# Delta rule: 32-row base inverse on GpSimd, one doubling level fewer on TensorE, and the second half's queries and keys projected earlier

## The chip, the cores and the metric

The kernel runs on one core of a Trainium2 chip. A core has TensorE (PE; its weight loads are listed as PEld), VectorE (DVE), ScalarE (ACT), GpSimd (POOL), a sync engine (SP) that issues most transfers, and 16 DMA engines. Each engine works through its own instructions in the order in which they stand and waits where a semaphore tells it to. The metric is the device time of one execution in microseconds; lower is better.

## The reference

Two transformer blocks in sequence over 256 tokens of width 2048, all in float32. The change lies in the second block's mixer, in its gated delta rule (8 heads of 128, token chunks of 64):

```python
A = jnp.where(tri_strict, jnp.einsum('bhnid,bhnjd->bhnij', kb, k) * decay, 0.0)
T = lax.linalg.triangular_solve(eye + A, jnp.broadcast_to(eye, A.shape),
                                left_side=True, lower=True)
u = jnp.einsum('bhnij,bhnjd->bhnid', T, v * beta[..., None])
w = jnp.einsum('bhnij,bhnjd->bhnid', T, kb * jnp.exp(G)[..., None])
...
v_new = u_i - jnp.einsum('bhck,bhkv->bhcv', w_i, state)
o_i = (jnp.einsum('bhck,bhkv->bhcv', q_i, state)
       + jnp.einsum('bhij,bhjv->bhiv', qk_i, v_new))
```

Here `q`, `k`, `v` come from one large projection `h @ w_in`, followed by a short causal convolution, silu and (for q and k) a norm; the delta rule's output is normed, gated, joined to the output of a block-sparse attention and multiplied by `w_out`.

## The kernel before

**Projections.** Every large matrix product goes through `linear` (L269). It splits each weight tile into a high and a low part (ACT L320, DVE L324) and adds three fp32r products of 128x512 (L295 to L297) for each of the two token halves. Weights stream from HBM through three buffers, issued by SP (L261, L265). The first token half is `LAG` units ahead of the second.

**Background work.** Everything small (convolutions, the delta rule, attention) is written as generators. `linear` advances them between its units: each `yield cost, wait` says how much of the budget a step takes and how long, on a planner's clock that counts projected columns, the lane must rest before its next step. `stat` of the last product `w_out` forces generators whose result it needs. The instructions then stand in a fixed order on each engine, so a background product on PE that is not ready holds back all projection products behind it.

**The delta rule.** Here the kernel treats 128 tokens as one chunk, and each half of the heads has four heads by two chunks, eight 128x128 lower triangular matrices to invert. `gdn(half)` makes convolutions of k and q, norms, then the masked products of k with k (`KE`, L1108 and L1109). `base_inverse` (L1017) inverts the diagonal blocks of 16 rows: POOL writes the blocks to a scratch in DRAM (eight transfers, L1025), reads them back with one block matrix per partition (`K`, 64 partitions of 16x16, L1034), scales them by `cb` (L1043), runs 15 elimination steps of two instructions (L1048, L1049) on `R`, writes `R` to DRAM (L1051) and reads it back into the diagonal of `T` (eight transfers, L1054). For each b in `LEVELS` = 16, 32, 64 a doubling level follows: POOL makes the mask `cm` (L1126), PE transposes `T` (8 matrices, L209 through `transpose8`), multiplies `KE` by `T` (L1131) and the transposed `T` by the masked result (L1137), and DVE subtracts (L1138). Then `finish(t)` gives the output of each token half: `head_norm` (ACT, DVE, ACT with a square root, DVE, POOL L1201 and L1203) and `tsplit` (four transposes on PE, L209).

**The order around it.** In `block2_mixer` (L1241) the projection calls, each 1024 columns wide, come as: q and k of half 0; v of half 0 and a gate; q and k of half 1; v of half 1 and attention queries; and so on to `w_out`. `gdn(0)` runs in lane 0 from the second of these on, `gdn_value(0)` (convolution and scaling of v) in lane 1 from the third on, and `gdn(1)` from the fourth on. `moba(half)` is the attention: its normed output goes through POOL L1201 as well. A row's line number shifts by one from L1048 on in the changed file.

Of the kernel before, what the change touches and what calls it, by code (L numbers as in the profile page):

```python
# [13 lines left out]
ALU = mybir.AluOpType  # L14
# [4 lines left out]
S, D, P = 256, 2048, 128  # L19
# [4 lines left out]
HP = 50  # L24
HPE = 30
HPL = 30
LEVELS = (16, 32, 64)
TWO_PI = 2.0 * math.pi


def constants():
# [8 lines left out]
    parts = [m > n, m <= n, m < n, np.ones((128, 128))]  # L40
    for b in LEVELS:
        c = np.arange(64)
# [100 lines left out]
class Net:  # L143
# [873 lines left out]
    def base_inverse(self, KE, cc):  # L1017

        nc = self.nc
        d1, d2 = self.scratch(64 * 256), self.scratch(64 * 256)  # L1020

        def view(d, b):
            return bass.AP(tensor=d.tensor, offset=d.offset + b * 256, ap=[[16, 16], [2048, 8], [1, 16]])
        for b in range(8):
            nc.gpsimd.dma_start(view(d1, b), KE[b * 16:b * 16 + 16, :, b * 16:b * 16 + 16])  # L1025
        tp = self.mis([P, P])
        nc.tensor.transpose(tp[:8, :], cc.rearrange("p t h -> p (t h)"), self.ident)
        cr = self.w2([8, P])
        nc.vector.tensor_scalar(cr, tp[:8, :], -1.0, None, op0=ALU.mult)
        yield 0.2, 4.0  # L1030
        cb = self.sm([64, 16], "cb", 1)
        nc.gpsimd.dma_start(cb, cr)
        K = self.w2([64, 16, 16])
        nc.gpsimd.dma_start(K.rearrange("p a b -> p (a b)"), bass.AP(tensor=d1.tensor, offset=d1.offset, ap=[[256, 64], [1, 256]]))  # L1034
        R = self.w2([64, 16, 16])
        Rf = R.rearrange("p a b -> p (a b)")
        e = nc.gpsimd
        e.memset(R, 0.0)
        e.memset(Rf[:, 0:256:17], 1.0)
        T = self.s4([P, 8, P])  # L1040
        e.memset(T, 0.0)
        yield 0.0, 4.0
        e.tensor_tensor(K, K, cb[:, None, :].to_broadcast([64, 16, 16]), op=ALU.mult)  # L1043
        yield 0.0, 1.0
        for m in range(15):
            sh = [64, 15 - m, m + 1]
            tmp = self.sm(sh, "btmp")
            e.tensor_tensor(tmp, K[:, m, m + 1:][:, :, None].to_broadcast(sh), R[:, m, :m + 1][:, None, :].to_broadcast(sh), op=ALU.mult)  # L1048
            e.tensor_tensor(R[:, m + 1:, :m + 1], R[:, m + 1:, :m + 1], tmp, op=ALU.add)  # L1049
        yield 0.0, 12.0  # L1050
        nc.gpsimd.dma_start(bass.AP(tensor=d2.tensor, offset=d2.offset, ap=[[256, 64], [1, 256]]), Rf)  # L1051
        yield 0.0, 3.5
        for b in range(8):
            nc.gpsimd.dma_start(T[b * 16:b * 16 + 16, :, b * 16:b * 16 + 16], view(d2, b))  # L1054
        yield 0.0, 4.5
        self.Tb = T

# [15 lines left out]
    def gdn(self, half, qraw, kraw, beta, decays, zs, at, box):  # L1073
# [48 lines left out]
        c8 = cc.rearrange("p t h -> p (t h)")[:, :, None].to_broadcast([P, 8, 64])  # L1122
        for li, b in enumerate(LEVELS):
            cm = self.w2([P, 8, 64])
# [115 lines left out]

    def block2_mixer(self):  # L1241
        nc, I = self.nc, self.I
        self.c2 = self.s4([P, 704])
        nc.sync.dma_start(self.c2, I["cst2"])
        parked = []
        stat = r = self.norm_split(self.piece, "mix", "rx", lambda x=self.x: parked.append(self.park(x)))
        self.piece = self.x = None
        w = I["w_in_2"][0]
        zs = [self.s4([P, 2, 512]) for _ in range(2)]
        ba = self.sm([P, 2, 16], "ba", 1)  # L1250

        def ev_z1(t, j, ps):
            if j == 0:
                nc.scalar.activation(zs[1][:, t, 0:264], ps, AF.Silu, scale=r[t])
                return
            nc.scalar.activation(zs[1][:, t, 264:512], ps[:, 0:248], AF.Silu, scale=r[t])
            nc.scalar.activation(ba[:, t], ps[:, 248:264], AF.Copy, scale=r[t])
        self.lpat = "v"
        self.linear(w, [(3584, 264), (3848, 264)], stat, ev_z1, carry=True)
        beta, g = self.gates(ba)  # L1260
        decays = {}
        bias = {}
        self.bg.add(self.moba_bias(bias), 1)
        self.bg.add(self.gdn_decay(0, g, decays), 0)
        oT = LazyAT(self)
        SC = 128.0 ** -0.5

        def to(*dst):
            def f(t, j, ps):
                d, kind = dst[j]  # L1270
                if kind == "t":
                    return self.channel_major(d, t, ps, r[t])
                elif kind == "q":
                    return self.channel_major(d, t, ps, r[t], SC)
                elif kind == "z":
                    nc.scalar.activation(d[:, t], ps, AF.Silu, scale=r[t])
                else:
                    nc.scalar.activation(d[:, t].rearrange("p h c -> p (h c)"), ps, AF.Copy, scale=r[t])
            return f

        def new():
            return self.s4([P, 4, S])
        q, k = new(), new()
        self.linear(w, [(0, 512), (1024, 512)], stat, to((q, "t"), (k, "t")), carry=True)
        box = {}
        self.bg.add(self.gdn(0, q, k, beta, decays, zs, oT, box), 0)
        v = new()
        self.linear(w, [(2048, 512), (3072, 512)], stat, to((v, "t"), (zs[0], "z")), budget=2.0, carry=True)
        self.bg.add(self.gdn_value(0, v, box), 1)
        q, k = new(), new()  # L1290
        self.linear(w, [(512, 512), (1536, 512)], stat, to((q, "t"), (k, "t")), budget=2.0, carry=True)
        box = {}
        self.bg.add(self.gdn_decay(1, g, decays), 0)
        self.bg.add(self.gdn(1, q, k, beta, decays, zs, oT, box), 0)
        v, mq = new(), new()
        self.linear(w, [(2560, 512), (4112, 512)], stat, to((v, "t"), (mq, "q")), budget=2.0, carry=True)
        self.bg.add(self.gdn_value(1, v, box), 1)
        mk, mv = new(), self.s4([P, 2, 4, P])
        self.linear(w, [(5136, 512), (6160, 512)], stat, to((mk, "t"), (mv, "v")), budget=2.0, carry=True)
# [287 lines left out]
```

## Time and profile before

| | us |
|---|---|
| median of 3 runs | 2434.64 |
| lowest and highest | 2433.32, 2436.43 |
| the profiled execution's own time | 2435.66 |
| its span | 2433.5 |
| PE busy | 2406.7 |
| DVE busy | 1553.0 |
| ACT busy | 1429.6 |
| POOL busy | 199.8 |

The profiled execution took 1.0 us more than the median, and 2.2 us lie outside its span. A busy time on PE is not the work itself: products are pipelined, and the distance from one start to the next is what a product costs. POOL is idle for most of the program, but the chain from `KE` to `T` runs through it.

### The profile page before, as it was taken

To read this page: it belongs to the slowest core of one execution; us is meant where nothing else is said; L and a number is where in the kernel's file an instruction comes from. 1 tells how busy PE (TensorE), PEld (TensorE's weight loads), DVE (VectorE), ACT (ScalarE), POOL (GpSimd) and SP (SyncE) were. 2 spreads that over 40 slices of the span, in tenths; PEclk is the share of its full clock that TensorE was granted. 3 is DMA by queue.
4 is the path that set the end of the run, shared out by engine and by line. 5 is a ranking of instruction groups with operands and counts; after the bars stand their busy time and mean duration, and the time that the engine had idled before them with its cause. 6 is when DMAs were issued, how large, how long until landed. Compare 5 with 4: busy or idle time off the path is not lost.

```text
span 2433.5 us, 32136 instructions
## 1 busy us (share of the span) xinstructions
PE 2406.7 (99%) x11363; PEld 1994.4 (82%) x11363; DVE 1553.0 (64%) x2842; ACT 1429.6 (59%) x2678; POOL 199.8 (8%) x217
## 2 busy tenths in 40 slices
PE   9999999999999999999999999999999999999998
PEld 7788878888888888888887888788888888888887
DVE  6998585555555666566758656576556556567754
ACT  7458675545545556466545555586565565566744
POOL 1740000000000000000301411000000000001000
PEclk9999999999999999999999999999999999999999
DMA  7546456555555666656444535645565555555553
GB/s 250 173 137 217 156 166 206 191 189 191 184 191 190 200 197 198 194 175 223 156 140 143 182 122 188 210 165 190 183 197 173 191 191 173 190 197 224 187 205 139
DMA packets 193569, 448.64 MB, mean 184 GB/s; under 512 B 12932, under 2 KB 17568, under 8 KB 193408
## 3 DMA queue, kind: packets, MB, share of 16 engines
q1 hardware_dynamic: 192192, 446.05, 55.1%
q8 instruction: 89, 1.46, 0.2%
q0 software_dynamic: 1216, 0.54, 0.1%
q14 instruction: 72, 0.59, 0.1%
HBM read 439.78 MB, written 6.75 MB: 183 GB/s over the span
## 4 chain that ended last, share of the span: by engine, by line
PE 90%; issue 3%; ACT 3%; DVE 2%; DMA 1%; POOL 0%; POOLq 0%; SPq 0%; ACTq 0%; DVEq 0%
PE acc L295 28%; PE acc L296 28%; PE acc L297 28%; PE mis L209 3%; ACT wh L320 1%; DVE wl L324 1%; DMA raw<-in_w_uq_dram 1%; PE mis L1108 0%; PE mis L1131 0%; PE mis L1137 0%; DVE s L984 0%; POOLq L1583 0%; ACT s L242 0%; ACT w L203 0%; DMA s<-in_mem_dram 0%
## 5 line engine op out<-in xcount | busy, mean ns | idle before, releaser
L324 DVE TENSOR_TENSOR wl<-raw,wh 128x512 fp32r<-128x512 f32 (+2 forms) x1574 | 1101.3, 708 | 763.3 <-ACT wh L320 759.1
L320 ACT ACTIVATE wh<-raw 128x512 fp32r<-128x512 f32 (+3 forms) x1640 | 1011.0, 625 | 859.4 <-DVE wl L324 480.1
L295 PE MATMUL acc<-wh,s 128*128 128x512 f32 (+3 forms) x3280 | 1284.1, 394 | 3.9 <-ACT w L555 2.0
L296 PE MATMUL acc<-wl,s 128*128 128x512 f32 (+3 forms) x3280 | 1269.9, 388 | 2.5 <-DVE wl L324 2.1
L297 PE MATMUL acc<-wh,s 128*128 128x512 f32 (+3 forms) x3280 | 1268.5, 388 | 0.2 <-DVE s L243 0.2
L295 PEld LDWEIGHTS acc<-wh,s 128*128 128x128 f32 x3280 | 617.5, 188 | 125.6 <-ACT s L242 5.6
L296 PEld LDWEIGHTS acc<-wl,s 128*128 128x128 f32 x3280 | 618.0, 188 | 123.1 <-DVE wl L324 6.8
L297 PEld LDWEIGHTS acc<-wh,s 128*128 128x128 f32 x3280 | 616.3, 188 | 125.1 <-DVE s L243 1.7
L515 DVE SCALAR_TENSOR_TENSOR s<-mis,cols,s 128x255 f32<-128x255 f32 (+29 forms) x240 | 93.1, 455 | 0.0
L324 POOL TENSOR_TENSOR wl<-raw,wh 128x512 fp32r<-128x512 f32 (+2 forms) x66 | 84.0, 1286 | 91.4 <-ACT wh L320 90.3
L1406 POOL TENSOR_TENSOR s<-s,s 128x1024 f32<-128x1024 f32 x11 | 32.7, 2975 | 663.2 <-ACT s L1405 663.2
L243 DVE SCALAR_TENSOR_TENSOR s<-mis,cols,s 128x128 fp32r<-128x128 f32 x212 | 66.4, 346 | 18.1 <-ACT s L242 16.2
L242 ACT ACTIVATE s<-mis,cols 128x128 fp32r<-128x128 f32 x212 | 69.6, 379 | 13.9 <-PE mis L209 7.9
L209 PE MATMUL mis<-c,w 128*128 128x128 f32 x456 | 71.9, 275 | 2.2 <-ACT w L1234 1.4
L209 PEld LDWEIGHTS mis<-c,w 128*128 128x128 f32 x456 | 56.4, 140 | 20.9 <-ACT w L1234 3.0
L209 PE MATMUL mis<-c,s 128*128 128x128 f32 x416 | 61.7, 277 | 4.3 <-DVE s L747 1.4
L209 PEld LDWEIGHTS mis<-c,s 128*128 128x128 f32 x416 | 50.2, 142 | 16.5 <-issue 2.6
L866 DVE TENSOR_TENSOR s<-s,s 128x512 fp32r<-128x512 f32 x88 | 58.9, 686 | 1.1 <-ACT s L865 1.1
L203 ACT ACTIVATE w<-s 128x512 f32<-128x512 f32 (+2 forms) x90 | 51.4, 573 | 8.5 <-DVE s L1436 6.2
L865 ACT ACTIVATE s<-s 128x512 fp32r<-128x512 f32 x88 | 52.3, 621 | 4.2 <-POOL s L1406 4.0
L350 POOL MEMSET w<- 128x128 f32 x3 | 0.5, 204 | 658.8 <-PE mis L209 658.8
L1238 ACT ACTIVATE s<-mis 128x512 f32<-128x512 f32 x68 | 39.9, 594 | 23.0 <-PE mis L209 23.0
(261 smaller groups left out, 881.4 us busy)
## 6 DMA issues: line engine op xcount, KB each, us to landing
raw<-in_w_gate_dram SPq DMA_DIRECT2D x176, 512.0 KB
raw<-in_w_up_dram SPq DMA_DIRECT2D x176, 512.0 KB
raw<-in_w_down_dram SPq DMA_DIRECT2D x88, 1024.0 KB
raw<-in_w_in_dram SPq DMA_DIRECT2D x126, 512.0 KB
raw<-in_w_out_dram SPq DMA_DIRECT2D x32, 1024.0 KB
raw<-in_w_in_dram SPq DMA_DIRECT2D x12, 1024.0 KB
raw<-in_w_xkv_dram SPq DMA_DIRECT2D x8, 1024.0 KB
raw<-in_w_uq_dram SPq DMA_DIRECT2D x6, 768.0 KB
```

What stands on the lines that cost most here:

```text
L203: self.nc.scalar.activation(junk, src, AF.Square, scale=scale, accum_out=acc)
L209: self.nc.tensor.transpose(ps[:, i, :], s, self.ident)
L242: nc.scalar.activation(hh, ps[:, j], AF.Copy, scale=g)
L243: nc.vector.scalar_tensor_tensor(l[:, q + j, tt], ps[:, j], g, hh.bitcast(F32), op0=ALU.mult, op1=ALU.subtract)
L295: nc.tensor.matmul(o, ah[:, tt], h, start=u == 0, stop=False)
L296: nc.tensor.matmul(o, ah[:, tt], l, start=False, stop=False)
L297: nc.tensor.matmul(o, al[:, tt], h, start=False, stop=u == nk - 1)
L320: nc.scalar.activation(h, r, AF.Copy)
L324: eng.tensor_tensor(l, r, h.bitcast(F32), op=ALU.subtract)
L515: nc.vector.scalar_tensor_tensor(y, u[j // 2][:, j % 2, :S - s], wc(30 - s, j), y, op0=ALU.mult, op1=ALU.add)
L865: nc.scalar.activation(hl[:, 0], src, AF.Copy)
L866: nc.vector.tensor_tensor(hl[:, 1], src, hl[:, 0].bitcast(F32), op=ALU.subtract)
```

## The change

The base inverse now works on blocks of 32 rows: 32 partitions that each hold a 32x32 block, 31 elimination steps of two instructions instead of 15, four transfers to the scratch and four back instead of eight and eight. `LEVELS` loses 16, so each half has two doubling levels instead of three. `K` and `R` come from the pool of large tiles and all steps share one temporary. The planner's wait after the elimination is 26.0 instead of 12.0. In `block2_mixer` the projection of half 1's q and k moves ahead of that of half 0's v and the gate.

```diff
-LEVELS = (16, 32, 64)
+LEVELS = (32, 64)
...
-        d1, d2 = self.scratch(64 * 256), self.scratch(64 * 256)
+        d1, d2 = self.scratch(32 * 1024), self.scratch(32 * 1024)
...
-        for b in range(8):
-            nc.gpsimd.dma_start(view(d1, b), KE[b * 16:b * 16 + 16, :, b * 16:b * 16 + 16])
+        for b in range(4):
+            nc.gpsimd.dma_start(view(d1, b), KE[b * 32:b * 32 + 32, :, b * 32:b * 32 + 32])
...
-        K = self.w2([64, 16, 16])
-        nc.gpsimd.dma_start(K.rearrange("p a b -> p (a b)"), bass.AP(tensor=d1.tensor, offset=d1.offset, ap=[[256, 64], [1, 256]]))
-        R = self.w2([64, 16, 16])
+        K = self.s4([32, 32, 32])
+        nc.gpsimd.dma_start(K.rearrange("p a b -> p (a b)"), bass.AP(tensor=d1.tensor, offset=d1.offset, ap=[[1024, 32], [1, 1024]]))
+        R = self.s4([32, 32, 32])
...
-        e.tensor_tensor(K, K, cb[:, None, :].to_broadcast([64, 16, 16]), op=ALU.mult)
+        e.tensor_tensor(K, K, cb[:, None, :].to_broadcast([32, 32, 32]), op=ALU.mult)
         yield 0.0, 1.0
-        for m in range(15):
-            sh = [64, 15 - m, m + 1]
-            tmp = self.sm(sh, "btmp")
+        part = self.w2([32, 256])
+        for m in range(31):
+            sh = [32, 31 - m, m + 1]
+            tmp = part[:, :sh[1] * sh[2]].rearrange("p (a b) -> p a b", b=sh[2])
             e.tensor_tensor(tmp, K[:, m, m + 1:][:, :, None].to_broadcast(sh), R[:, m, :m + 1][:, None, :].to_broadcast(sh), op=ALU.mult)
             e.tensor_tensor(R[:, m + 1:, :m + 1], R[:, m + 1:, :m + 1], tmp, op=ALU.add)
-        yield 0.0, 12.0
+        yield 0.0, 26.0
...
-        for b in range(8):
-            nc.gpsimd.dma_start(T[b * 16:b * 16 + 16, :, b * 16:b * 16 + 16], view(d2, b))
+        for b in range(4):
+            nc.gpsimd.dma_start(T[b * 32:b * 32 + 32, :, b * 32:b * 32 + 32], view(d2, b))
...
         self.bg.add(self.gdn(0, q, k, beta, decays, zs, oT, box), 0)
+        q, k = new(), new()
+        self.linear(w, [(512, 512), (1536, 512)], stat, to((q, "t"), (k, "t")), budget=2.0, carry=True)
         v = new()
         self.linear(w, [(2048, 512), (3072, 512)], stat, to((v, "t"), (zs[0], "z")), budget=2.0, carry=True)
         self.bg.add(self.gdn_value(0, v, box), 1)
-        q, k = new(), new()
-        self.linear(w, [(512, 512), (1536, 512)], stat, to((q, "t"), (k, "t")), budget=2.0, carry=True)
```

On PE, the first doubling of half 0 stands in the kernel before as follows (`acc` are projection sums, `s_2572` is `T`, `s_2534` is `KE`); the product L1131 is the first that uses `T` beside its transposes:

```order
L297 MATMUL acc_2607_11455<-wh_11598,s_2261_9956 128x512
L209 MATMUL mis_11675<-c_81,s_2572_11322 128x128 x4
L209 MATMUL mis_11681<-c_81,s_2572_11322 128x128 x4
L1131 MATMUL mis_11687<-s_2572_11322,s_2534_11156 128x64 x8
L295 MATMUL acc_2605_11453<-wh_11698,s_2262_9957 128x512
```

In the changed kernel the same place on PE (`s_2573` is `T`, `s_2535` is `KE`, L1132 the old L1131):

```order
L297 MATMUL acc_2596_11477<-wh_11704,s_2263_9958 128x512
L209 MATMUL mis_11774<-c_81,s_2573_11319 128x128 x4
L209 MATMUL mis_11780<-c_81,s_2573_11319 128x128 x4
L1132 MATMUL mis_11786<-s_2573_11319,s_2535_11157 128x64 x8
L295 MATMUL acc_2594_11475<-wh_11797,s_2264_9959 128x512
```

Between the first product for `KE` and these transposes stood 192 projection products in the kernel before; now 252 stand there. The small blocks between them are the same in number. In half 1 there were 198 and are 267.

On POOL, half 1 of the kernel before: the elimination ends, `T` is filled, and only then come the mask and the two norms of the attention's output (`s_2975`, L1201):

```order
L1048 TENSOR_TENSOR btmp_13032<-w_2932_12926,w_2933_12928 64x15
L1049 TENSOR_TENSOR w_2933_12928<-w_2933_12928,btmp_13032 64x15
L1051 DMA scr_12801<-w_2933_12928 64x256
L1054 DMA s_2934_12931<-scr_12801 16x8x16 x8
L1126 TENSOR_TENSOR w_3056_13390<-s_2257_9951,gcc_12751 128x512
L1201 TENSOR_TENSOR s_2975_13090<-s_2975_13090,hrr_13369 128x512
L1201 TENSOR_TENSOR s_2975_13090<-s_2975_13090,hrr_13377 128x512
```

In the changed kernel (`w_2976` is the temporary, `s_2935` is `R`, `s_2939` the attention's output, L1202 the old L1201) the norms stand within the elimination, after 22 of its 31 steps:

```order
L1049 TENSOR_TENSOR w_2976_13131<-s_2934_12992,s_2935_12994 32x220
L1050 TENSOR_TENSOR s_2935_12994<-s_2935_12994,w_2976_13131 32x10x22
L1202 TENSOR_TENSOR s_2939_13014<-s_2939_13014,hrr_13348 128x512
L1049 TENSOR_TENSOR w_2976_13131<-s_2934_12992,s_2935_12994 32x207
L1202 TENSOR_TENSOR s_2939_13014<-s_2939_13014,hrr_13356 128x512
L1050 TENSOR_TENSOR s_2935_12994<-s_2935_12994,w_2976_13131 32x9x23
L1049 TENSOR_TENSOR w_2976_13131<-s_2934_12992,s_2935_12994 32x192
```

So nine elimination steps and the filling of `T` now stand behind a wait for the attention. In half 0 one mask (L1127, the old L1126) stands within the elimination in the same way. At the end of the mixer, half 1's last output products moved too, on PE, into the attention's products of half 1 (L796 to L798 and L1213, L1214 are attention; L1164 and L1165 are `finish(1)`; the transposes of `w_3129` belong to `finish(0)`):

```order
L798 MATMUL mis_14002<-s_3064_13578,w_3172_14000 128x128
L209 MATMUL mis_14008<-c_81,w_3129_13869 128x128 x4
L1213 MATMUL mis_14041<-s_2925_12975,s_2924_12974 128x128
L1214 MATMUL mis_14041<-s_2925_12975,s_2924_12974 128x256
L1164 MATMUL mis_14055<-s_3113_13798,s_2888_12792 128x128
L1165 MATMUL mis_14055<-s_3113_13798,s_2887_12791 128x128
```

In the kernel before they stood 125 projection products earlier, clear of the attention:

```order
L209 MATMUL mis_13869<-c_81,w_3147_13806 128x128 x4
L295 MATMUL acc_3124_13716<-wh_13880,s_2262_9957 128x512
...
L297 MATMUL acc_3125_13717<-wh_13849,s_2263_9958 128x512
L1163 MATMUL mis_13890<-s_3129_13727,s_2896_12755 128x128
L1164 MATMUL mis_13890<-s_3129_13727,s_2895_12754 128x128
```

The transposes of `finish(1)`'s output follow 17 projection products, six attention products, two score products and six transposes later.

## Rows read from the trace of the kernel before

**Rows 1.** The page: span, busy time of each engine, and the chain of work that ended last by engine.

```profile
span 2433.5 us, 32136 instructions
...
PE 2406.7 (99%) x11363; PEld 1994.4 (82%) x11363; DVE 1553.0 (64%) x2842; ACT 1429.6 (59%) x2678; POOL 199.8 (8%) x217
...
PE 90%; issue 3%; ACT 3%; DVE 2%; DMA 1%; POOL 0%; POOLq 0%; SPq 0%; ACTq 0%; DVEq 0%
```

**Rows 2.** Who PE waited for between 1100 and 1600 us, the stretch of the second block's mixer: us in total, times, longest.

```profile
PE mis L209 <- POOL s L1201: 1.2, 2, 0.8
```

**Rows 3.** Timeline of PE around the first doubling of half 0: start, duration, engine, line, operation, count.

```profile
1228.03 1.04 PE L209 MATMUL mis<-c,s 128*128 128x128 f32 x8
1228.90 1.90 PE L1131 MATMUL mis<-s,s 128*128 128x64 f32 x16
1230.61 0.48 PE L295 MATMUL acc<-wh,s 128*128 128x512 f32 x1
1230.93 0.39 PE L296 MATMUL acc<-wl,s 128*128 128x512 f32 x1
1231.16 0.39 PE L297 MATMUL acc<-wh,s 128*128 128x512 f32 x1
...
1233.42 1.89 PE L1137 MATMUL mis<-w,s 128*128 128x64 f32 x16
1235.12 0.48 PE L295 MATMUL acc<-wh,s 128*128 128x512 f32 x1
```

**Rows 4.** Timeline of POOL in half 0's base inverse: start, duration, line, operation, partitions x elements; in brackets the idle time before and what ended it.

```profile
1180.08 4.36 POOL L1025 DMA_DIRECT2D scr<-s  x8 [48.65 <-DVE s L1109]
...
1193.90 0.71 POOL L1043 TENSOR_TENSOR w<-w,cb 64x256 f32<-64x256 f32 x1 [3.85 <-DMA w<-scr]
1194.70 0.74 POOL L1048 TENSOR_TENSOR btmp<-w,w 64x15 f32<-64x15 f32 x1
1195.52 0.22 POOL L1049 TENSOR_TENSOR w<-w,btmp 64x15 f32<-64x15 f32 x1
1195.82 0.23 POOL L1048 TENSOR_TENSOR btmp<-w,w 64x28 f32<-64x28 f32 x1
...
1201.82 0.94 POOL L1041 MEMSET s<- 128x1024 f32 x1
...
1203.33 0.29 POOL L1048 TENSOR_TENSOR btmp<-w,w 64x63 f32<-64x63 f32 x1
1203.70 0.30 POOL L1049 TENSOR_TENSOR w<-w,btmp 64x63 f32<-64x63 f32 x1
...
1208.30 0.69 POOL L1049 TENSOR_TENSOR w<-w,btmp 64x28 f32<-64x28 f32 x1
...
1209.70 0.21 POOL L1049 TENSOR_TENSOR w<-w,btmp 64x15 f32<-64x15 f32 x1
1210.21 0.57 POOL L1051 DMA_DIRECT2D scr<-w  x1 [0.30 <-POOL w L1049]
1214.81 4.19 POOL L1054 DMA_DIRECT2D s<-scr  x8 [4.03 <-DMA scr<-w]
1219.01 3.06 POOL L1126 TENSOR_TENSOR w<-s,gcc 128x512 f32<-128x512 f32 x3
```

**Rows 5.** The same in half 1: PE's first products for `KE`, then POOL's first transfer, first and last elimination instruction.

```profile
1346.96 1.95 PE L1108 MATMUL mis<-s 128*128 128x128 f32 x16
...
1350.47 4.21 POOL L1025 DMA_DIRECT2D scr<-s  x8 [37.88 <-DVE grq L1155]
...
1362.52 0.21 POOL L1048 TENSOR_TENSOR btmp<-w,w 64x15 f32<-64x15 f32 x1
...
1376.90 0.21 POOL L1049 TENSOR_TENSOR w<-w,btmp 64x15 f32<-64x15 f32 x1
```

**Rows 6.** DVE beside the elimination: the busy time and number of L324 alone in the two stretches of elimination (first to last instruction), and one piece of DVE's timeline.

```profile
1194.70:1209.91 15.21, 7.74 (x11) 0.00 (x0) 1.00 0.44 140
1362.52:1377.11 14.59, 7.12 (x10) 0.00 (x0) 1.00 0.47 155
...
1208.21 1.34 DVE L324 TENSOR_TENSOR wl<-raw,wh 128x512 fp32r<-128x512 f32 x2 [1.09 <-ACT wh L320]
```

**Rows 7.** Line L1054, the transfers that fill `T`: time from issue to landing.

```profile
DMA to landing us min/median/max: 1.9/2.9/5.0
```

**Rows 8.** An earlier place (first block) where PE stood still: PE's timeline, and the busy time by stretch with the granted clock as the number behind POOL's.

```profile
169.59 0.69 PE L295 MATMUL acc<-wh,s 128*128 128x384 f32 x1 [2.04 <-ACT w L555]
...
169.28:172.70 3.42, 3.10 (x10) 2.99 (x11) 1.55 (x5) 3.39 (x10) 1.38 (x2) 0.50 0.65 163
```

**Rows 9.** Timelines of PE, POOL and ACT for norms that follow products: half 0's attention (last product, norms on POOL), half 1's `finish(1)` (last product, last norm instruction), and the end of half 1's attention (a table load on ACT, and the transposes that waited).

```profile
1405.48 0.39 PE L798 MATMUL mis<-s,w 128*128 128x128 f32 x2
1411.05 2.49 POOL L1201 TENSOR_TENSOR s<-s,hrr 128x512 f32<-128x512 f32 x2 [11.39 <-DVE hrr L1200]
...
1466.37 0.39 PE L1164 MATMUL mis<-s,s 128*128 128x128 f32 x2
1470.96 1.61 POOL L1203 TENSOR_TENSOR w<-w,s 128x512 f32<-128x512 f32 x1
...
1510.03 1.28 ACT L1198 ACT_TABLE_LOAD   x1
1514.45 0.66 PE L209 MATMUL mis<-c,s 128*128 128x128 f32 x4 [0.79 <-POOL s L1201]
```

More of the change, by code (lines that the diff above doesn't have):

```diff
@@ L1019, in base_inverse @@
         nc = self.nc
-        d1, d2 = self.scratch(64 * 256), self.scratch(64 * 256)
+        d1, d2 = self.scratch(32 * 1024), self.scratch(32 * 1024)
         def view(d, b):
-            return bass.AP(tensor=d.tensor, offset=d.offset + b * 256, ap=[[16, 16], [2048, 8], [1, 16]])
-        for b in range(8):
-            nc.gpsimd.dma_start(view(d1, b), KE[b * 16:b * 16 + 16, :, b * 16:b * 16 + 16])
+            return bass.AP(tensor=d.tensor, offset=d.offset + b * 1024, ap=[[32, 32], [4096, 8], [1, 32]])
+        for b in range(4):
+            nc.gpsimd.dma_start(view(d1, b), KE[b * 32:b * 32 + 32, :, b * 32:b * 32 + 32])
         tp = self.mis([P, P])
@@ L1030, in base_inverse @@
         yield 0.2, 4.0
-        cb = self.sm([64, 16], "cb", 1)
+        cb = self.sm([32, 32], "cb", 1)
         nc.gpsimd.dma_start(cb, cr)
-        K = self.w2([64, 16, 16])
-        nc.gpsimd.dma_start(K.rearrange("p a b -> p (a b)"), bass.AP(tensor=d1.tensor, offset=d1.offset, ap=[[256, 64], [1, 256]]))
-        R = self.w2([64, 16, 16])
+        K = self.s4([32, 32, 32])
+        nc.gpsimd.dma_start(K.rearrange("p a b -> p (a b)"), bass.AP(tensor=d1.tensor, offset=d1.offset, ap=[[1024, 32], [1, 1024]]))
+        R = self.s4([32, 32, 32])
         Rf = R.rearrange("p a b -> p (a b)")
@@ L1038, in base_inverse @@
         e.memset(R, 0.0)
-        e.memset(Rf[:, 0:256:17], 1.0)
+        e.memset(Rf[:, 0:1024:33], 1.0)
         T = self.s4([P, 8, P])
@@ L1042, in base_inverse @@
         yield 0.0, 4.0
-        e.tensor_tensor(K, K, cb[:, None, :].to_broadcast([64, 16, 16]), op=ALU.mult)
+        e.tensor_tensor(K, K, cb[:, None, :].to_broadcast([32, 32, 32]), op=ALU.mult)
         yield 0.0, 1.0
-        for m in range(15):
-            sh = [64, 15 - m, m + 1]
-            tmp = self.sm(sh, "btmp")
+        part = self.w2([32, 256])
+        for m in range(31):
+            sh = [32, 31 - m, m + 1]
+            tmp = part[:, :sh[1] * sh[2]].rearrange("p (a b) -> p a b", b=sh[2])
             e.tensor_tensor(tmp, K[:, m, m + 1:][:, :, None].to_broadcast(sh), R[:, m, :m + 1][:, None, :].to_broadcast(sh), op=ALU.mult)
             e.tensor_tensor(R[:, m + 1:, :m + 1], R[:, m + 1:, :m + 1], tmp, op=ALU.add)
-        yield 0.0, 12.0
-        nc.gpsimd.dma_start(bass.AP(tensor=d2.tensor, offset=d2.offset, ap=[[256, 64], [1, 256]]), Rf)
+        yield 0.0, 26.0
+        nc.gpsimd.dma_start(bass.AP(tensor=d2.tensor, offset=d2.offset, ap=[[1024, 32], [1, 1024]]), Rf)
         yield 0.0, 3.5
-        for b in range(8):
-            nc.gpsimd.dma_start(T[b * 16:b * 16 + 16, :, b * 16:b * 16 + 16], view(d2, b))
+        for b in range(4):
+            nc.gpsimd.dma_start(T[b * 32:b * 32 + 32, :, b * 32:b * 32 + 32], view(d2, b))
         yield 0.0, 4.5
@@ L1242, in block2_mixer @@
         nc, I = self.nc, self.I
-        self.c2 = self.s4([P, 704])
+        self.c2 = self.s4([P, 640])
         nc.sync.dma_start(self.c2, I["cst2"])
```

## The prediction

> **What bounds the kernel now.** I read the page's parts 1 and 4 first [rows 1]: PE is busy for 2406.7 of 2433.5 us and is 90% of the chain that ended last, so time is gained by taking work off PE and lost by making PE wait. The list of waits comes next: in the whole mixer of the second block the longest entry is 1.2 us in two waits on POOL [rows 2]. So the background work is hidden there, but only because each piece stands on PE late enough. The third view is the timeline of POOL along the chain from `KE` to `T` [rows 4, 5], laid beside PE's timeline [rows 3]: POOL issues the last transfer into `T` at about 1218.5 us (1214.81 + 7 x 0.53), it lands after some 2.9 us [rows 7], and PE takes `T` at 1228.03. The slack was 6.6 us. That number decides this change.
>
> **PE work removed.** One doubling level is eight transposes (1228.03 to 1228.90, 0.87 us), L1131 (to 1230.61, 1.71) and L1137 (1233.42 to 1235.12, 1.70): 4.28 us. The first projection product behind each of its two blocks takes 0.32 instead of 0.23, which adds 0.18 [rows 3]. That is 4.46 a level, one level in each half: **-8.9 us**. The DVE and ACT work of the level goes too; neither engine sets the end, so I count it as nothing. The smaller constant (64 columns less, once, under projection work) is nothing as well.
>
> **POOL work added.** A step m on blocks of n rows has (n-1-m)(m+1) elements in each of its two instructions. Over all steps that is 680 elements for 16 rows and 5456 for 32. An undisturbed instruction on 15 elements takes 0.22 us with 0.08 to the next start (1195.52, 0.22, next at 1195.82) [rows 4]; without 0.03 for its elements that is 0.27 fixed. For the price of an element I have 28 and 63 elements at 0.23 and 0.29 in L1048 (1.7 ns), 15 and 63 at 0.22 and 0.30 in L1049 (1.7 ns), L1043 at 256 elements in 0.71 (2.0 ns) and L1126 at 512 in 1.02 (1.6 ns) [rows 4]. L1126 spreads one operand over its row as L1048 does, L1043 reads two whole tiles as L1049 does, so I take 1.65 and 2.0 ns, 3.65 for the pair. Undisturbed, 31 steps are 62 x 0.27 = 16.7 and 5456 x 3.65 ns = 19.9, together 36.6 us; 15 steps would be 30 x 0.27 + 680 x 3.65 ns = 10.6.
>
> They took more: 1194.70 to 1209.91 without the 0.94 memset is 14.3 us [rows 4], and 1362.52 to 1377.11 without its memset 13.6 [rows 5]. The extra 3.0 to 3.7 us, 24% of the time, falls on instructions that run beside DVE's L324: L1049 on 28 elements takes 0.69 at 1208.30 where an undisturbed one of 28 takes 0.23, and DVE's L324 has run since 1208.21 [rows 4, 6]. L324 is busy for half of both stretches, 7.74 of 15.21 and 7.12 of 14.59 us [rows 6], and goes on at that pace as long as PE does. So I price the extra by time: 36.6 / 0.76 = **48 us**. The bounds are 36.6 (no collisions) and, if they went by instruction, 36.6 + 62 x 0.11 = 44; upward 36.6 / 0.67 = 55, should instructions with more elements lose two thirds of L324's half of the time.
>
> [...]
>
> **Half 0: when `T` is there, and when PE wants it.** The chain starts at 1180.08 as before. To the first step it took 14.6 us; four transfers fewer save 4 x 0.53 = 2.1, and scaling 1024 instead of 256 elements adds 768 x 2.0 ns = 1.5: 14.0. The two larger memsets lie in the 3.85 us wait for `K` [rows 4]. The steps take 48, and the mask that now stands within them 1.1. Behind the steps it took 1209.91 to 1221.4, 11.5 us; four transfers fewer leave 9.4. `T` is there at 1180.1 + 14.0 + 49.1 + 9.4 = 1252.6. PE has 60 more projection products ahead of it, 60 x 0.227 = 13.6 us [rows 3], and arrives at 1241.6. The wait is 11 us; once PE stops, L324 stops soon after and POOL's last steps run freely, so I take **+10 us** (0 with the loop of 36.6, 6 with 44, 17 with 55). Queued behind that wait are all projection products of PE; ACT and DVE run out of buffers a little later.
>
> A stop has a second price. In the first block PE stood still for 2.04 us until 169.59, and from 169.28 to 172.70 the granted clock was 0.50, the lower of the two levels [rows 8]. Half speed for 3.4 us loses **+1.7 us**, and I add it for this wait.
>
> **Half 1.** Let P be the time of the first product for `KE`. By the prices above and its order, PE reaches the attention's transposes at P + 58 and `T` at P + 77 (267 products are 60.6 us, the background between them the rest). POOL has 22 of 31 steps done at about P + 52: 3.5 to the start (1346.96 to 1350.47), 12.1 to the steps [rows 5], and 44 x 0.27 + 4301 x 3.65 ns = 27.6, over 0.76 36. Then it must wait for the attention's norm, which is ready 5.3 us after the last attention product (1405.7 to 1411.05) [rows 9]; that product now stands at P + 53, so P + 58. Two norms of 1.04 with one step's half between end at P + 61. PE had no wait at this place and now waits for both, **+2.4 us**. The nine steps left take 9.1 / 0.76 = 12, the tail 9.4: `T` is there at P + 82, and PE, 2.4 later than before, arrives at P + 79.6: **+2.5 us** (0 to 5).
>
> **The end of the mixer.** `finish(1)` needs 6.1 us from its last product (1466.5) to its last norm (1472.57), and a square root among exponentials adds a table load of 1.28 on ACT [rows 9], 7.4 together. The order leaves 6.5 us of PE work between. The next exponential needs a load again. I take 1 for each, **+2 us** (0 to 5). The waits of 1.2 us that PE already had here stay.
>
> **What I cost at nothing.** The swapped projections are the same products; the transposes and copies that end them stand the same distance behind. The convolution of v in half 0 comes later, and its transposes stand 34 products and 2.6 us of level work behind the projection, 10 us against the 38 products (8.6 us) behind which PE did not wait before [rows 2]. Two large tiles more are held for some 50 us; transfers on SP that wait for a tile of POOL's stand well behind the loop's end. If one of these covers failed, each would cost 1 to 3 us.
>
> **The sum.** -8.9 + 10 + 1.7 + 2.4 + 2.5 + 2 = +9.7 us on the profiled execution's 2435.66, which is 1.0 above the median: 2445.4, or 2444 beside the median of 2434.64.
>
> **Rivals.** *A: the loop is hidden.* If collisions stay as few as they were in number, or cost long instructions no more than short ones, or the planner's 26 us is near the truth, `T` arrives by 1241.6 and no clock drop follows. What is left is -8.9 + 2.4 + 1 = -5.5, 2429; with every wait gone -8.9, 2426. For it: the slack grew by 13.6 us. Against it: even the undisturbed rows give 36.6, so a gain needs a loop of at most 40 us in both halves. *B: the loss is counted by instruction.* The loop takes 44, half 0 waits 6: the sum is +5.7 with the clock, 2440, and without the clock drop or the end's 2 us 2438, no change. *C: long instructions collide worse.* With a loop of 55 half 0 waits 17, half 1 5, each with 1.7: -8.9 + 17 + 5 + 3.4 + 4.4 = +21, 2455. For it: each L324 can then meet data instead of the fixed part. The point that decides between a gain and a loss is a loop of about 41 us.
>
> **How the numbers follow.** The kernel's runs differ by 0.1%, so a change under 0.2%, 4.9 us, can't be told from none: below 2429.8 is faster, above 2439.5 slower. Forecast 0.45; A 0.20; B 0.22; C 0.13. Faster is most of A: 0.17. No change is most of B and the rest of A: 0.27. Slower 0.56. The range runs from A to C, 2428 to 2456.
>
> **What would show it.** In the changed kernel's profile: a gap on PE before half 0's first doubling, with the transfers into `T` as the releaser, and a stretch of granted clock 0.50 behind it; L1049 and L1050 together over some 48 us, with instructions near 0.6 us for 256 elements and 1.0 to 1.2 beside L324; 64 instead of 96 products in L1132; waits of PE on POOL's L1202 in half 1. The forecast is wrong if the loop takes under 41 us, or if PE arrives at `T` much later than 1241.6.

## The result, and the profile after

The changed kernel takes 2448.09 us (median of 4 runs, 2447.55 to 2449.67) against 2434.41 for the kernel before in the same comparison: ratio 1.0055, 95% interval 1.0044 to 1.0067, 13.7 us slower. The profiled execution has a span of 2446.5 us, 13.0 more than before. First the page: span, busy time by engine, chain that ended last.

```profile
span 2446.5 us, 31995 instructions
...
PE 2405.8 (98%) x11283; PEld 1989.8 (81%) x11283; DVE 1557.8 (64%) x2838; ACT 1431.2 (59%) x2676; POOL 256.4 (10%) x263
...
PE 86%; DVE 4%; POOL 3%; issue 3%; ACT 2%; DMA 2%; POOLq 0%; SPq 0%; ACTq 0%; DVEq 0%
```

PE has 80 matmuls fewer than in [rows 1] and yet is busy for the same time: work went, and the work that stayed ran slower somewhere. PE's share of the chain fell from 90% to 86%; DVE, POOL and DMA have more of it. The list of PE's waits between 1100 and 1600 us says where (us in total, times, longest):

```profile
PE mis L209 <- DMA s<-scr: 11.5, 2, 7.7
PE mis L209 <- POOL s L1202: 2.7, 4, 1.1
PE mis L209 <- POOL w L1204: 0.9, 1, 0.9
```

In [rows 2] the longest was 1.2 us in two waits. Now the transposes of `T` wait twice, 11.5 us in sum, for the transfers that fill it. POOL's timeline in half 0, beside [rows 4], from its first transfer to the last:

```profile
1177.60 2.48 POOL L1025 DMA_DIRECT2D scr<-s  x4 [48.64 <-DVE s L1110]
...
1186.66 2.37 POOL L1043 TENSOR_TENSOR s<-s,cb 32x1024 f32<-32x1024 f32 x1 [0.92 <-DMA s<-scr]
1189.11 0.57 POOL L1049 TENSOR_TENSOR w<-s,s 32x31 f32<-32x31 f32 x1
...
1213.95 0.61 POOL L1049 TENSOR_TENSOR w<-s,s 32x256 f32<-32x256 f32 x1
1214.64 1.07 POOL L1050 TENSOR_TENSOR s<-s,w 32x256 f32<-32x256 f32 x1
1215.79 0.96 POOL L1049 TENSOR_TENSOR w<-s,s 32x255 f32<-32x255 f32 x1
...
1239.46 0.24 POOL L1050 TENSOR_TENSOR s<-s,w 32x31 f32<-32x31 f32 x1
1240.00 0.55 POOL L1052 DMA_DIRECT2D scr<-s  x1 [0.30 <-POOL s L1050]
1242.52 2.32 POOL L1055 DMA_DIRECT2D s<-scr  x4 [1.98 <-DMA scr<-s]
```

The loop runs from 1189.11 to 1239.70; without the mask of 1.0 us that stands in it, 49.6 us. Its 62 instructions are busy for 44.9 us of that (L1049, then L1050):

```profile
1189.11:1239.70 50.59, 21.64 (x31) 1.00 0.54 180
...
1189.11:1239.70 50.59, 23.28 (x31) 1.00 0.54 180
```

Almost the same instruction takes 0.61 or 0.96 us. DVE's timeline beside it:

```profile
1214.01 1.11 DVE L324 TENSOR_TENSOR wl<-raw,wh 128x512 fp32r<-128x512 f32 x1 [0.67 <-ACT wh L320]
1215.37 0.90 DVE L324 TENSOR_TENSOR wl<-raw,wh 128x512 fp32r<-128x512 f32 x1 [0.25 <-ACT wh L320]
1216.73 0.69 DVE L324 TENSOR_TENSOR wl<-raw,wh 128x512 fp32r<-128x512 f32 x1 [0.46 <-ACT wh L320]
```

L1049 at 1213.95 began before L324 and took 0.61, and L324 1.11 instead of 0.69; at 1215.79 L324 was already running, and L1049 took 0.96. PE's timeline where `T` is wanted, in half 0 and in half 1:

```profile
1246.84 1.94 PE L209 MATMUL mis<-c,s 128*128 128x128 f32 x8 [7.70 <-DMA s<-scr]
1248.57 3.51 PE L1132 MATMUL mis<-s,s 128*128 128x64 f32 x16
1251.84 0.77 PE L295 MATMUL acc<-wh,s 128*128 128x512 f32 x1
...
1445.08 1.94 PE L209 MATMUL mis<-c,s 128*128 128x128 f32 x8 [3.82 <-DMA s<-scr]
1446.81 3.52 PE L1132 MATMUL mis<-s,s 128*128 128x64 f32 x16
```

PE stands for 7.70 and 3.82 us. And then it is slow: the eight transposes take 1.94 us where they took 1.04 [rows 3]. The busy time by stretch shows why; the number behind POOL's is the granted clock:

```profile
169.28:172.70 3.42, 3.42 (x22) 3.42 (x21) 2.38 (x7) 3.41 (x11) 0.62 (x1) 1.00 0.71 224
1242.37:1246.84 4.47, 0.00 (x0) 0.03 (x1) 0.00 (x0) 0.00 (x0) 3.38 (x5) 0.50 0.70 247
1246.84:1256.02 9.18, 9.18 (x34) 8.31 (x35) 1.26 (x2) 1.83 (x3) 0.00 (x0) 0.50 0.00 0
1445.07:1453.99 8.92, 8.91 (x35) 8.22 (x36) 0.99 (x2) 1.93 (x4) 0.00 (x0) 0.50 0.01 2
```

The clock fell to 0.50, the lower of the two values (1.00 and 0.50) that the clock's records of these two executions hold, 3.6 us after PE's last start in half 0, and came back only 9.2 us after PE had work again; 8.9 us in half 1. In these two stretches PE is 100% busy and is slow: projection products start 0.43 us apart (from 1252.42 on) instead of 0.23 (from 1233.77 on). Counted as half speed, the granted 0.50, the 18.1 us lose 9.05. The first row has another use: the stretch that was slow in the profiled execution before [rows 8] is at full clock here, so 1.7 of that execution's 2433.5 us are chance and not this place. Of the twelve kernels below, which are the same there, two show it, and not the one that waited longest: from start to start PE stood for 2.38 us there in the kernel before and for 1.94 in e6, both with the slow stretch, and for 2.54 in e3 and 1.50 in the changed kernel, both without.

The account, from starts on PE: -8.9 of work; +7.85 (8.08 between two starts at half 0's `T` instead of 0.23) and +4.6 for the low clock behind it; +1.9 for two waits for the attention's norms; +4.0 and +4.5 at half 1's `T`; +1.0 at the mixer's end. That is +15.0, less the 1.7 of chance +13.3, against 13.0 in the spans.

### The profile page after: what moved, and what is told of

Read it like the earlier page. It is cut to its first block, busy times and chain, and to the rows that moved or that the text cites. A ratio compares the mean times of both kernels' runs of the same rounds, so it can differ in the third digit from the quotient of the medians.

```text
span 2446.5 us, 31995 instructions
## 1 busy us (share of the span) xinstructions
PE 2405.8 (98%) x11283; PEld 1989.8 (81%) x11283; DVE 1557.8 (64%) x2838; ACT 1431.2 (59%) x2676; POOL 256.4 (10%) x263
## 4 chain that ended last, share of the span: by engine, by line
PE 86%; DVE 4%; POOL 3%; issue 3%; ACT 2%; DMA 2%; POOLq 0%; SPq 0%; ACTq 0%; DVEq 0%
PE acc L295 27%; PE acc L296 27%; PE acc L297 27%; PE mis L209 3%; POOL s L1050 1%; POOL w L1049 1%; DVE wl L324 1%; DVE s L984 1%; ACT wh L320 1%; DVE s L515 0%; DMA s<-scr 0%; PE mis L1132 0%; DMA raw<-in_w_uq_dram 0%; DVE s L979 0%; POOLq L1584 0%
## 5 line engine op out<-in xcount | busy, mean ns | idle before, releaser
L324 DVE TENSOR_TENSOR wl<-raw,wh 128x512 fp32r<-128x512 f32 (+2 forms) x1574 | 1108.6, 713 | 765.6 <-ACT wh L320 759.7
L324 POOL TENSOR_TENSOR wl<-raw,wh 128x512 fp32r<-128x512 f32 (+2 forms) x66 | 84.0, 1287 | 89.2 <-ACT wh L320 84.9
L209 PE MATMUL mis<-c,s 128*128 128x128 f32 x400 | 61.5, 283 | 17.2 <-DMA s<-scr 11.5
L209 PEld LDWEIGHTS mis<-c,w 128*128 128x128 f32 x456 | 56.5, 141 | 20.3 <-POOL w L1204 1.5
```

The costliest lines, as they stand in the source:

```text
L209: self.nc.tensor.transpose(ps[:, i, :], s, self.ident)
L324: eng.tensor_tensor(l, r, h.bitcast(F32), op=ALU.subtract)
```

## The experiments

Theory T: PE waits for a late `T`, because GpSimd's loop got longer than the time until PE wants `T`, and each wait drags a stretch of half clock behind it. Its main rival was the other half of the change, the new order of projections. Each experiment (e1 to e12) was timed against the kernel before (medians 2434.3 to 2435.0).

### One part at a time

Only the new order, with 16-row blocks and three levels (e1):

```diff
+        q, k = new(), new()
+        self.linear(w, [(512, 512), (1536, 512)], stat, to((q, "t"), (k, "t")), budget=2.0, carry=True)
         v = new()
         self.linear(w, [(2048, 512), (3072, 512)], stat, to((v, "t"), (zs[0], "z")), budget=2.0, carry=True)
         self.bg.add(self.gdn_value(0, v, box), 1)
-        q, k = new(), new()
-        self.linear(w, [(512, 512), (1536, 512)], stat, to((q, "t"), (k, "t")), budget=2.0, carry=True)
```

> The kernel before with the second half's queries and keys ahead of the first half's values, and nothing else; blocks of 16 rows and three doublings stay. Theory T (the loss is PE waiting for a late T, and the low granted clock that follows each wait): POOL's loop stays 14 us, T is there before PE in half 0 (slack 6.6 us), so the time stays within 2434 +/- 3 and no gap of more than 1.5 us stands ahead of a doubling. Rival R (the new order itself costs, by background work that is pressed together in half 1 and at the end of the mixer): 2438 to 2442.

Measured: 2434.21 us, ratio 0.9999 (0.9990 to 1.0009). The longest wait of PE in the mixer is 0.8 us:

```profile
PE mis L209 <- POOL s L1201: 2.0, 4, 0.8
```

With 16-row blocks the order costs nothing; rival R, that the order costs by itself, is out.

Only the 32-row base (e2: the diff above taken back from the changed kernel):

> The changed kernel with the old order of the two projections; 32-row base and two doublings stay. Theory T: PE still stands 60 products later at T in half 0 and its gap there is 7 to 9 us, in half 1 3 to 8 us with the norms' waits of the attention, each followed by granted clock 0.50: 2446 to 2452. Rival R: without the new order the time falls to 2434 to 2440.

Measured: 2442.45 us, ratio 1.0033 (1.0020 to 1.0046), between what the two theories gave, and the list of PE's waits says something that neither had:

```profile
PE acc L296 <- DVE wl L324: 8.3, 2, 8.1
PE mis L209 <- POOL s L1202: 5.6, 3, 4.3
```

In half 0 PE stands for 8.1 us, but not for `T`: for a product's operand from DVE. DVE's timeline there, under POOL's loop:

```profile
1209.96 2.90 DVE L979 TENSOR_SCALAR s<-s,cols 128x256 f32<-128x256 f32 x4
1212.78 9.58 DVE L984 SCALAR_TENSOR_TENSOR s<-s,cols,s 128x255 f32<-128x255 f32 x12
```

The same block on DVE in the kernel before, where it began as the shorter loop ended (1209.91 [rows 4]):

```profile
1209.47 1.13 DVE L979 TENSOR_SCALAR s<-s,cols 128x256 f32<-128x256 f32 x4
1210.52 4.81 DVE L984 SCALAR_TENSOR_TENSOR s<-s,cols,s 128x255 f32<-128x255 f32 x12
```

The convolution of v takes 12.4 us in place of 5.9; DVE's order has no L324 between, and PE runs dry. So the long loop does a second harm, to DVE, and the new order keeps v's convolution out of it (in the changed kernel it begins at 1271.77, behind the loop). The traces show it from both engines: L984, which reads two tiles, takes 0.48 us alone and 0.88 in the median beside the loop, and in the two pairs of L1049 and L324 above the one that began later was the longer (L324 with 1.11 against 0.61 us, then L1049 with 0.96 against 0.90). By what the two hold each other up is not shown.

The other wait in e2's list, 4.3 us in half 1, is for an attention norm that stands on POOL behind the longer loop, and it has a low clock behind it too:

```profile
1418.54:1424.34 5.80, 5.80 (x18) 4.82 (x19) 3.63 (x4) 2.16 (x4) 4.86 (x6) 0.50 0.28 83
```

e2 also answers what the order did within the change as it was made: with the 32-row base and a wait of 26 the new order is 5.6 us slower than the old one (2448.09 against 2442.45). In e2 PE is held up ahead of `T`, in half 0 for L324 and in half 1 for the norm, and comes to `T` (at 1250.1 and 1437.6 us) after the transfers into it, last issued by 1244.8 and 1422.7; it has no wait for `T`, and it runs at half clock for 3.0 and 5.8 us instead of 9.2 and 8.9, which is 4.7 of the 5.6 us.

### What the half clock costs

PE works through the wait, on transposes that nobody reads (e3):

```diff
         T = self.Tb
+        for _ in range(18 - 9 * half):
+            self.transposes([KE[:, h] for h in range(4)])
```

> The changed kernel with transposes of KE into unused PSUM tiles ahead of T's own transposes: 72 in half 0 and 36 in half 1, their results read by nobody, about 7.8 and 3.9 us of PE work at the full clock. They stand where PE waited. Theory T: T is as late as before, so the wait itself is not won back, but PE doesn't stand still, the granted clock stays at 1.00 and the products behind T start at full speed: 4.5 us less in half 0 and 4.4 in half 1, together 2439 (2437 to 2442). Rival S (the low clock costs next to nothing, since ACT or DVE or a full queue would hold PE up behind the wait anyway): 2447 to 2450.

Measured: 2440.72 us, ratio 1.0028 (1.0018 to 1.0038), 7.4 us less than the changed kernel. The expected 9 were not quite reached, but the reading is plain: 72 added and 8 real transposes in one row, the doubling's products at full speed behind them, the clock (second fence, busy time by stretch) at 1.00.

```profile
1240.46 8.90 PE L209 MATMUL mis<-c,s 128*128 128x128 f32 x80
1249.19 1.90 PE L1134 MATMUL mis<-s,s 128*128 128x64 f32 x16
```

```profile
1246.50:1256.00 9.50, 9.50 (x74) 8.90 (x72) 2.41 (x4) 2.35 (x4) 0.85 (x1) 1.00 0.06 15
```

PE does 108 transposes more than in the changed kernel, and the kernel is faster. Rival S, by which the low clock costs next to nothing, is out.

What comes first behind the wait was changed in another run (e12): a yield between `T`'s transposes and the first doubling's products lets twelve projection products in.

```diff
             TT = self.transpose8(T)
+            if li == 0:
+                yield 0.8, 1.8
             ps = self.mis([P, 8, 64])
```

> The changed kernel with a yield between T's eight transposes and the first doubling's sixteen 64-column products, so that twelve projection products of 512 columns stand between them in both halves. The gap ahead of T stays as it is (8.1 and 4.2 us), and PE's work too. Theory L (how long the clock stays low behind a wait depends on what PE is given then: in the changed kernel the 64-column products come first and the clock rises 9 us after PE resumed, behind waits for L324 projection products come first and it rises after 3 to 4 us): the low stretches shrink from 13.65 and 10.24 us to 10 and 7 or less, PE loses 1.5 us or more less behind each wait: 2443 to 2446. Rival M (the length of the wait sets it): 13.65 and 10.24 us again, 2447 to 2449.

Measured: 2447.28 us, ratio 1.0050 (1.0033 to 1.0067): the time is not told apart from the changed kernel's. It lies above theory L's 2443 to 2446, in rival M's 2447 to 2449. The clock, though, did what theory L said, and in half 1 more than it said:

```profile
1250.01:1255.12 5.11, 5.11 (x16) 4.38 (x17) 0.00 (x0) 1.77 (x3) 0.00 (x0) 0.50 0.00 0
...
1446.77:1449.67 2.90, 2.90 (x11) 2.71 (x12) 0.00 (x0) 1.19 (x2) 0.00 (x0) 0.50 0.02 6
```

Behind the same gaps (8.4 and 4.3 us) PE ran at half clock for 5.1 and 2.9 us instead of 9.2 and 8.9, 5.0 us less lost. The profiled execution gave some 2 of it back in gaps at the mixer's end, where half 1 now comes later, and had the chance stretch of [rows 8] as well (1.7). So the length of the wait alone does not set the clock's return, and rival M is out as an account of the clock. The mean granted clock of a whole execution bears that out beyond the one profile: 0.996 in all four, 0.995 in all four of the changed kernel. But the saving did not reach the total, and theory L's price for it is not shown by the time.

### Making T late no more

The planner waits longer behind the elimination, in half 0 alone (e4):

```diff
...
-        yield 0.0, 26.0
+        yield 0.0, 34.0 if half == 0 else 26.0
...
```

> The changed kernel with the planner's wait behind the elimination raised from 26 to 34 in half 0 alone: PE finds T's first transposes 300 instead of 252 products behind the first product for KE, some 10.9 us later. Theory T: half 0's gap of 8.1 us and its low clock (4.5 us) go, -12.6; half 1's own gap shrinks, since its T's transposes stand 897 instead of 879 products from there, but its last products stand at the mixer's end (0 to +4 us): 2432 to 2440. Rival P (POOL's loop slows DVE's L324 and so PE, whether or not PE waits at T): the gap moves but no more than 3 us are won, 2445 to 2448.

Measured: 2433.47 us, ratio 0.9995 (0.9985 to 1.0004), 14.6 us less than the changed kernel, as theory T had it. Rival P, by which the loop slows PE whether or not PE waits for `T`, is out: POOL's loop is nearly as long as before (48.9 us from its first to its last instruction, 49.6 in the changed kernel without the mask), and PE is at 14.00 of 14.00 us between 1242 and 1256 at full clock. Half 1, now later, pays for part of it near the mixer's end, in waits (PE's list) and in 3.4 us of half clock behind one of them:

```profile
PE mis L796 <- ACT w L794: 2.9, 2, 2.2
PE mis L209 <- POOL s L1202: 1.4, 2, 0.8
PE mis L209 <- ACT s L986: 1.4, 1, 1.4
PE mis L209 <- DMA s<-scr: 1.3, 1, 1.3
```

The same wait with the old order of projections, that is, e2 with the diff of e4 (e6):

> The old order of the projections with the 32-row base and the planner's wait of half 0 raised to 34; it differs from e4 by the order alone. Theory D (in the base-only kernel PE's 8.5 us gap of half 0 was no wait for T: the convolution of v, twelve DVE instructions in a row, ran inside POOL's loop, took 0.80 us each instead of 0.48, and kept L324 away from PE): T standing later doesn't help, the gap ahead of an L296 stays at 7 to 9 us and the time at 2438 to 2443. Rival W (that gap was T's lateness in another place): it goes, 2432 to 2435 as in e4.

Measured: 2442.28 us, ratio 1.0032 (1.0020 to 1.0043); PE's wait for L324 is 7.1 us, L984 takes 0.88 us in the median.

```profile
PE acc L296 <- DVE wl L324: 7.7, 2, 7.1
```

Theory D holds: that gap was DVE's. Beside e4 the new order gains 8.8 us here, where it was worth nothing in e1 and cost 5.6 beside e2: what it is worth hangs on whether PE waits for `T`.

The same again (e7), with a wait of 30 ahead of v's convolution, by which DVE's order puts L324s between its instructions:

```diff
         nc = self.nc
+        if half == 0:
+            yield 0.0, 30.0
         yield from self.gdn_conv(vraw, 16 + half * 4)
```

> As e6, with a wait of 30 ahead of the first half's convolution of v: in DVE's order its sixteen instructions now stand in ones to fives between L324s instead of all in a row; they still run inside POOL's loop. Theory D: each still takes some 0.8 us, but L324 is never held for more than 4 or 5 us and PE's products in stock cover that: the gap falls from 8 to under 2 us, 2432 to 2436. Rival B (the busy DVE is short of time inside the loop however it is arranged): gaps of 5 us and more in sum, 2437 to 2442.

Measured: 2437.40 us, ratio 1.0012 (1.0002 to 1.0021): within rival B's range, 1.4 us above theory D's. The waits, 3.9 us in sum, lie between the two. L984 still takes 0.84 us in the median (798 to 952 ns), but e6's wait of 7.1 us became four of 0.7 to 1.0 us in its place. Of e6's 8.8 us against e4, 4.9 are gone and 3.9 remain: the block in a row does somewhat more than half of the harm, and the rest is there however the block is spread.

The loop halved, so that `T` comes sooner and is no longer the inverse, to see whether the loop's length alone decides (e9):

```diff
             e.tensor_tensor(tmp, K[:, m, m + 1:][:, :, None].to_broadcast(sh), R[:, m, :m + 1][:, None, :].to_broadcast(sh), op=ALU.mult)
-            e.tensor_tensor(R[:, m + 1:, :m + 1], R[:, m + 1:, :m + 1], tmp, op=ALU.add)
+            if m == 30:
+                e.tensor_tensor(R[:, m + 1:, :m + 1], R[:, m + 1:, :m + 1], tmp, op=ALU.add)
```

> The changed kernel without the additions of the first 30 of the 31 elimination steps (32 instructions on GpSimd instead of 62, so T is not the inverse); PE's order, the planner's waits and the two projections stand as in the changed kernel. Theory T: the loop takes some 24 us instead of 50, T is there 18 us before PE in half 0 and about as early in half 1, both gaps (8.1 and 4.2 us), both stretches at half clock (some 4.5 us each) and the attention's waits of 2.3 us go: 2448 - 23 = 2425 (2423 to 2429). Rival U (part of the 13.7 us comes from the pressed background work, whatever POOL does): 2430 and more.

Measured: 2428.14 us, ratio 0.9975 (0.9965 to 0.9984). The loop takes 24.3 us in half 0. With the order of PE as in the changed kernel, neither first doubling waits for `T`, and no stretch of the mixer is at half clock. The loop's length carries 20 of the changed kernel's us. About 3 us less than theory T's 23 came back; the waits that remain are those of the attention's norms (2.0 us in sum) and two of 0.9:

```profile
PE mis L209 <- POOL s L1203: 2.0, 3, 0.8
PE acc L296 <- DVE wl L324: 0.9, 1, 0.9
PE mis L209 <- POOL w L1205: 0.9, 1, 0.9
```

### Half 1, and kernels that beat both

```diff
-        self.bg.add(self.gdn_decay(1, g, decays), 0)
-        self.bg.add(self.gdn(1, q, k, beta, decays, zs, oT, box), 0)
+        self.bg.add(self.gdn_decay(1, g, decays), 2)
+        self.bg.add(self.gdn(1, q, k, beta, decays, zs, oT, box), 2)
```

Lane 2 lets half 1 begin while half 0 ends. With nothing else changed (e10):

> The changed kernel with the second half's delta rule in a lane of its own and the planner's waits left at 26. It starts 102 products earlier against the projections, so the attention's norms come behind its loop on GpSimd and its last products no longer stand at the mixer's end; PE's first product for T stands 258 products behind its KE (267 before). Theory T: half 0 keeps its gap of 8 us and the low clock behind it; half 1 loses the norms' 2.3 us and the end's 1 us, and its own gap of 4 us and its low clock stay or shrink by what the norms held POOL up: 2434 to 2444.

Measured: 2446.77 us, ratio 1.0049 (1.0036 to 1.0063): a miss. The norms' waits went, as expected, but PE came to `T` nine products sooner, and the gap there grew from 4.2 to 5.4 us, with 7.6 us of half clock behind it. PE's waits:

```profile
PE mis L209 <- DMA s<-scr: 12.7, 2, 7.7
PE mis L209 <- POOL s L1202: 1.2, 2, 0.8
```

Room that isn't given to the planner's wait helps nothing. With both, lane 2 and waits of 34 (half 0) and 30 (half 1) (e5):

> The changed kernel with longer planner waits behind the elimination (34 in half 0, 30 in half 1), and the second half's delta rule in a lane of its own, so that it no longer queues behind the first half's: its first product for KE stands 522 products behind half 0's (612 in the changed kernel), its T's transposes 282 products later (267), its last products 933 behind half 0's first (1058 and more). Theory T: no gap over 1.5 us ahead of either first doubling, no granted clock 0.50 in the mixer, the attention's norms and the mixer's end wait no longer than before the change, and the work taken off PE is all kept: 2434.5 - 8.9 = 2426 (2424 to 2430). Rival Q (POOL's longer loop costs PE something wherever it stands, by slowing DVE): 2431 to 2436.

Measured: 2428.45 us, ratio 0.9976 (0.9966 to 0.9986). PE no longer waits for `T` in either half. What keeps it from 2426 is in half 0's end, whose norms on POOL now meet half 1's work (L1202 takes 2.33 us at 1299 and 1.04 at 1315): 3.3 us of waits, and one stretch of 3.4 us at half clock behind the longer of them, which theory T had not expected. The profiled execution, at 2430.85 us, was the slowest of the nine.

```profile
PE mis L209 <- POOL w L1204: 3.3, 2, 2.0
PE mis L209 <- POOL s L1202: 1.6, 3, 0.8
```

Last, the loop on the other engine, handed over in small pieces, with lane 2 kept (e8):

```diff
+        e = nc.vector
         for m in range(31):
...
+            if m % 2:
+                yield 0.0, 1.3
-        yield 0.0, 26.0
+        yield 0.0, 7.0
```

> The changed kernel with the elimination's 62 instructions on DVE instead of GpSimd, two steps handed over per unit of projection and 7 waited at the end (so that T's transposes stand 270 instead of 252 products behind the first product for KE), and the second half in a lane of its own as in e5. Theory T with POOL's price per element as the cause of the lateness: DVE's L324 takes 0.60 us for 512 elements, 1.2 ns an element, so 62 x 0.1 + 10912 x 1.2 ns = 19 us of DVE, half of whose time is free there: the loop is spread over the 20 us that the planner gives it or a little more, T is there before PE, and 2426 to 2431 follows. Rival V (DVE's own backlog then makes L324 late): PE waits for L324 in several places, 2434 to 2442.

Measured: 2427.47 us, ratio 0.9974 (0.9964 to 0.9984). The loop's two instructions on DVE, busy time between 1201 and 1236 us (first row the product, second the addition), and in the second fence the longest waits of PE:

```profile
1201.00:1236.00 35.00, 10.16 (x31) 1.00 0.55 179
...
1201.00:1236.00 35.00, 10.18 (x31) 1.00 0.55 179
```

```profile
PE mis L209 <- POOL w L1207: 1.8, 2, 1.5
PE mis L1153 <- DVE w L1179: 1.6, 1, 1.6
```

62 instructions are busy for 20.3 us in place of 44.9 (19 expected; the 0.1 us an instruction in that sum was my estimate, and no run shows it by itself), and no product waits for L324, though DVE is busy for 9.72 of 10 us between 1220 and 1230. With two more waits of the planner raised at half 0's end (e11):

```diff
-        yield 1.2, 2.6
+        yield 1.2, 5.0 if half == 0 else 2.6
...
-            yield 2.0, 6.0
+            yield 2.0, 8.5 if half == 0 else 6.0
```

> The kernel of e8 (loop on DVE, second half in its own lane) with two planner waits of the first half's end raised, 2.6 to 5.0 ahead of the second chunk's products and 6.0 to 8.5 ahead of the normed transposes, where PE still had gaps of 2.0 and 1.9 us. Theory T: these 3 to 4 us go, 2424 to 2426, the level of the removed work alone. Rival G (the order has moved something else into a wait): 2427 to 2430.

Measured: 2424.65 us, ratio 0.9964 (0.9952 to 0.9977), 10.2 us less than the kernel before and 23.4 less than the changed one. Three of its five runs lie at 2424.6, two at 2427.5 and 2428.5, in rival G's range, so its gain on e8 (2426.35 to 2430.29) is not sure. The longest wait left in the mixer is 1.6 us for a norm on POOL.

## Why the prediction was right, and where it wasn't

The forecast was 2444 us and slower, the measurement 2448. The mechanism it named decided: e9 takes the wait for `T` away and the loss with it. Step by step:

- *PE work removed, -8.9.* The runs without waits for `T` bear out its size, though each differs in more than the level: -6.7 (e9, where norms are still waited for) and -10.2 (e11, which has half 1 in a lane of its own).
- *The loop, 48 us.* 49.6. The sum that priced the collisions by time came nearest; by instruction (rival B) it would have been 44, and 55 for rival C.
- *Half 0's wait, +10.* +7.85. PE's arrival was right to 0.1 us (61.4 us behind the chain's start, 61.5 said). `T` came 3.3 us sooner than said: `K` landed after a wait of 0.9 us instead of 3.9 [rows 4], and the read-back was issued after 2.0 instead of 4.0, against 1.6 more for the loop.
- *The clock, +1.7.* This is the term that was mis-sized: +9.1. Two errors made it. I took it over from a single place [rows 8] where PE stood for 2 us and the clock was back after 3.4, a stretch that is there by chance, in three of the fourteen profiled executions; and I counted it for half 0 alone in the forecast, though half 1 had a wait of its own in it. e3 measures it from the other side: 7.4 us come back when PE doesn't stand still.
- *Half 1.* Norms +2.4, measured +1.9. `T` +2.5 (0 to 5), measured +4.0; the terms that I gave, `T` at P + 82.4 and PE at P + 79.4, make it 3.0 rather than 2.5.
- *The end, +2.* +1.0, in a wait for a norm on POOL (L1204).
- *Costed at nothing.* The new order is worth nothing by itself (e1), as said. What I did not see is that it protects DVE from the longer loop (8.8 us, e4 and e6), and yet costs 5.6 us as long as PE waits for `T` (e2): I had asked what L324 does to POOL, not what POOL does to DVE.

The errors partly cancelled: the sum of +9.7 missed the account's +15.0 by 5.3: 7.4 too little for the clock and 1.5 for half 1's `T`, against 2.2 too much for half 0's wait, 0.5 for the norms and 1.0 for the end. So the direction was understood and the size owes something to luck; the stated range of 28 us would have held most outcomes. Rivals: A (hidden) would have needed a loop below about 41 us; e9 with its shorter loop landed at 2428.1, in A's 2426 to 2429. B would have needed 44 us for the loop and C 55; it took 49.6.

Still open: why the total in e12 did not follow the clock, beyond the gaps that its one profile shows at the mixer's end.

## What to carry to other kernels

Work that is moved from the bounding engine to a slow one is free only while its result is there before it is asked for: compare the chain's length with the distance at which the consumer stands, in the consumer's own work, and move the consumer along with it (34 instead of 26 here was worth 14.6 us). Price a stall on TensorE at the wait plus the half clock behind it, for each wait, and read that from the granted clock; here it doubled the loss in half 1 (4.0 us of wait, 4.5 of half clock). And look at both sides where two engines run beside each other: what the longer work suffers (L1049 0.96 us instead of 0.61), and what it does to its neighbours (L984 0.88 us instead of 0.48).

## What the runs showed of the hardware

- The half clock after a stall can last longer than the stall: 9.2 us of PE's work behind a wait of 7.7, 8.9 behind one of 3.8; 3.1 behind one of 2.0 [rows 8]. With twelve projection products between `T`'s transposes and the 64-column products it was 5.1 behind a wait of 8.0 and 2.9 behind one of 3.9 (e12); and 108 transposes whose results nobody reads made the kernel 7.4 us faster (e3).
- GpSimd's loop slowed DVE: twelve two-input instructions took 0.88 us each instead of 0.48 (e2), four with one tensor input 2.90 us together instead of 1.13.
- The same elimination keeps DVE busy for 20.3 us (e8) and GpSimd for 44.9, or 49.6 from its first start to its last end without the mask that stands in it.
